# Own tiles, an early load and a new order around the rounding of the delta-rule outputs in a bidirectional hybrid block

## The chip, the cores and the metric

The kernel runs on one core of a Trainium2 chip. The metric is the device time of one execution in microseconds (us), given as the median of several runs. The engines are named as in the profile: PE is the matrix engine (TensorE), with PEld for its weight loads; DVE is VectorE, ACT is ScalarE, POOL is GpSimd, SP is SyncE. SP, ACT and POOL each have a queue in which they issue DMA transfers; in the profile, SPq and ACTq rows are such issues, while those of POOL stand under POOL. Every engine works through its own list of instructions in order. Where an instruction waits, everything behind it on that engine waits too.

## What is computed

The block takes 256 tokens of width 2048 (one sequence, one layer). It is an adaptive layer norm with a projection into two branches, a merge, an output projection and a gated feed-forward layer, all in float32. The part around the change, cut from the reference:

```python
mod = c_act @ ada_w + ada_b
shift_m, scale_m, gate_m, shift_f, scale_f, gate_f = jnp.split(mod[:, None, :], 6, axis=-1)
h = rms_norm(x, norm_mix_w) * (1 + scale_m) + shift_m
proj = h @ w_in
...
h_a = bidirectional(mlstm_chunkwise, (q_a, k_a, v_a), (log_i[0], log_f[0]), (log_i[1], log_f[1]))
h_a = rms_norm(h_a.transpose(0, 2, 1, 3), mlstm_norm_w.reshape(A_HEADS, A_DV)).reshape(bsz, t, A_V)
y_a = (jax.nn.sigmoid(a_o.astype(f32)) * h_a).astype(x.dtype) @ w_branch_a
...
o_b = bidirectional(gated_delta_chunkwise, (q_b, k_b, v_b), (beta[0], log_decay[0]), (beta[1], log_decay[1]))
o_b = rms_norm(o_b.transpose(0, 2, 1, 3), gdn_norm_w.reshape(B_HEADS, B_DV)).reshape(bsz, t, B_V)
y_b = (o_b * jax.nn.silu(b_z.astype(f32))).astype(x.dtype) @ w_branch_b

g_a, g_b = jnp.split(jax.nn.sigmoid(merge), N_BRANCH, axis=-1)
x = x + gate_m * ((g_a * y_a + g_b * y_b) @ w_out)
```

The mLSTM branch has 4 heads (keys of 256, values of 512), the gated delta rule 16 heads of 128.

## The kernel before

**Matmuls in two parts.** Every large weight is split into a rounded high part and a rest, `wh` and `wl`, and so is every activation (`hh` and `hl`, `obh` and `obl`, and so on). A product then takes three matmuls: high by high, low by high, high by low. ACT rounds (`wh`), DVE subtracts (`wl`). `tjob` (line 195) does this for weights with tokens as rows of the output: it loads 1 MB of weights per step `u` into one of three `raw` buffers by a DMA on SP, makes two halves of `wh` and `wl` of 128x1024 each (three buffers for each tag), and issues twelve matmuls per half (lines 230 to 232). Each call gives back control after each half, and so is a list of small pieces of work. `fjob` (line 169) does the same with tokens along the free axis.

**Filling.** The delta rule is a chain of small dependent steps. Its function `gdn_phase2` (line 745) handles a pair of heads and gives back control after each step; between the steps `fill` (line 265) and `stream` (line 883) issue pieces of the projections, so that PE has work. The adaLN products (`add`, line 118: one DVE instruction over 128x2048 for a block of `mod`) are dealt out in the same way.

**Planner and pins.** The instructions are traced in the order of the program. A scheduler then orders each engine's list by its own estimate of when an instruction's inputs are there and its buffers free, program order being the priority. So an instruction that stands later in the program may come earlier on its engine. `order(ins)` (line 72) pins one instruction behind the one traced before it on the same engine.

**Corrected outputs.** The last step of `gdn_phase2` transposes a pair's normalised outputs back (line 837), scales them into a tile `obt` of 128x256 (lines 840 and 841, ACT), and stores it to `ob_d` in DRAM by a DMA on ACT's queue (line 842). `obt` uses the tag "evf" of the pool `evp`, with two buffers; the evictions of the mLSTM's q and k (`keep_f`, line 355: `ev_a`, stored to `kq_d`) use the same two.

**mLSTM.** `mlstm(h)` (line 911) loads decays and q, k of a head (lines 915 and 917, POOL's queue), computes the scores and the decay matrix (lines 921 to 944; `psc` is the scores' product, line 930), then the denominators (line 958), and then the products by v for two blocks of 128 tokens (`ph`, line 974). For each token block and head there are three products, each of them two records in the trace; they go into two PSUM tiles of a tag `g` with four buffers. ACT scales the first (line 976), DVE adds the second (line 977), ACT squares and sums (line 978).

**The changeover.** After the last pair of the delta rule its pool `bk` is freed (line 1060). Pools of the next stage are opened in its place. Line 1116 loads the corrected outputs of groups 0 and 1, each 512 KB, by POOL's queue into two buffers `o4` of the pool `ml`. Then heads 0 and 1 of the mLSTM are driven on by `next(cores)`; `o_split` (line 1075) rounds a group's outputs into `obh` (ACT, 128x1024) and subtracts into `obl` (DVE), both pinned. The order by the program is: denominators; rounding of group 0, load of group 2, products by v of token block 0; rounding of group 1, load of group 3, products of token block 1; rounding of group 2. The branch projection `y_b` (line 1079) consumes group `g` in its weight step `u = g`. It begins with the load of a merge gate (`gtb`, 512 KB, line 1081, SP's queue, two buffers), which is read after its last matmul.

Of the kernel before, what the change touches and what calls it, by code (L numbers as in the profile page):

```python
# [9 lines left out]
F32 = mybir.dt.float32  # L10
F32R = mybir.dt.float32r
AF = mybir.ActivationFunctionType
ALU = mybir.AluOpType
PSUM = bass.MemoryType.PSUM

P = 128
T = 256
# [35 lines left out]
def hybrid_block(ctx: ExitStack, tc: tile.TileContext, xr, nfr, crow, pk_d, cst_d, ada2, ada4, win0, winb, wint, wba, wbb, wo, wgu, wd, out, dbg=None):  # L53
    nc = tc.nc
    V, S, G, PE = nc.vector, nc.scalar, nc.gpsimd, nc.tensor

    def pool(stack, name, bufs=1, **kw):
        return stack.enter_context(tc.tile_pool(name=name, bufs=bufs, **kw))
# [3 lines left out]
    rows_p = pool(ctx, "rows")  # L62
    acc_ps = pool(ctx, "acc_ps", 4, space=PSUM)
    g_ps = pool(ctx, "g_ps", 4, space=PSUM)
    sa, sx, sf = ExitStack(), ExitStack(), ExitStack()
    crp = pool(ctx, "crp")
    bigA = pool(sa, "bigA", 2, side="right")

# [3 lines left out]
    def order(ins, yes=True):  # L72

        return tc.keep_in_program_order(ins) if yes else ins

    def gps(name):
        return g_ps.tile([P, 512], F32, tag="g", name=name)
# [60 lines left out]
    def settle(keep=0, only=None):  # L138

        now = [f for f in behind if only is None or f.__name__ == only]  # L140
        for f in now[: len(now) - keep]:
            behind.remove(f)
            f()
# [143 lines left out]
    mb_d = [tc.dram_tile([P, 2, 512], F32, name=f"mb_d{g}") for g in range(4)]  # L287
    ob_d = [tc.dram_tile([4, P, T], F32, name=f"ob_d{g}") for g in range(4)]
# [6 lines left out]
    evp = pool(sa, "evp", side="right")  # L295
# [193 lines left out]
    with ExitStack() as s0:  # L489
        w0 = pool(s0, "w0")  # L490

        x = w0.tile([P, KB, T], F32, name="x")
        ss = w0.tile([P, 2], F32, name="ssx")
# [73 lines left out]
            fill(2 if i in (2, 3, 4, 6, 8, 9, 10) else 1)  # L567


    bk = pool(sx, "bk")  # L570
    own, nxt, half = cst[:, CS_OWN : CS_OWN + 4], cst[:, CS_NEXT : CS_NEXT + 4], cst[:, CS_HALF : CS_HALF + 2]
    even, odd = cst[:, CS_EVEN : CS_EVEN + 1], cst[:, CS_ODD : CS_ODD + 1]
# [172 lines left out]
    def gdn_phase2(g, p):  # L745
# [3 lines left out]
        hs = slice(2 * p, 2 * p + 2)  # L749
# [84 lines left out]
        for e, on in enumerate(ons):  # L834
            h, hl_ = 4 * g + 2 * p + e, 2 * p + e
            for t in range(2):
                PE.transpose(px[:, (2 * e + t) * P : (2 * e + t + 1) * P], on[:, t], ident)
        for e in range(2):
            h, hl_ = 4 * g + 2 * p + e, 2 * p + e
            obt = evp.tile([P, T], F32, tag="evf", bufs=2, name=f"obt{h}")  # L840
            S.activation(obt, px[:, e * T : (e + 1) * T], AF.Copy, scale=pk[:, PK_GNW + h : PK_GNW + h + 1])
            S.dma_start(ob_d[g][hl_], obt)
        yield
# [39 lines left out]
    def stream(h0):  # L883

        todo = []

        def piece():

            for q in list(todo):
                q[0] -= 1  # L890
                if not q[0]:
                    todo.remove(q)
                    next(heads1[q[1]])

        for h in range(h0, min(h0 + 2, NH_B)):
            for j in range(3):
                for _ in b_job(h, j):
                    piece()
                    yield True
            todo += [[2, h], [4, h]]  # L900
        while todo:
            fill(1)
            piece()
            yield True
        while True:
            fill(1)
            yield True

    mq, sq_ = {}, ExitStack()

    def mlstm(h):
        mp, load = mq["pool"], G
        bc = mp.tile([P, 2, T], F32, tag="bc", bufs=2, name=f"bc{h}")
# [45 lines left out]
        dn = ml.tile([P, 2, 2], F32, tag="dn", bufs=2, name=f"dn{h}")  # L959
# [4 lines left out]
        hs = ml.tile([P, 2, DV_A], F32, tag="hs", bufs=2, name=f"hs{h}")  # L964
        sq = ml.tile([P, DV_A], F32, tag="sqh", bufs=2, name=f"sqh{h}")
        ss = ml.tile([P, 2], F32, tag="ssh", bufs=2, name=f"ssh{h}")
        yield
        for t in range(2):
            pn = []
            for d in range(2):  # L970
                ph = gps(f"ph{h}_{t}_{d}")
                terms = src[d, t]
                for i, (w, s) in enumerate(terms):
                    PE.matmul(ph, w, vt[:, s], start=i == 0, stop=i == len(terms) - 1)
                pn.append(ph)
            S.activation(hs[:, t], pn[0], AF.Copy, scale=dn[:, t, 0:1])
            V.scalar_tensor_tensor(hs[:, t], pn[1], dn[:, t, 1:2], hs[:, t], ALU.mult, ALU.add)
            S.activation(sq, hs[:, t], AF.Square, accum_out=ss[:, t : t + 1])
            yield
        S.activation(ss, ss, AF.Sqrt, bias=epsc, scale=1.0 / DV_A)  # L980
        V.reciprocal(ss, ss)
# [3 lines left out]
        for e2 in range(2):  # L985
            px = gps(f"pxa{h}_{e2}")
            for e in range(2):
                f = 2 * e2 + e
# [33 lines left out]
    for g in range(4):  # L1022
        blocks = gdn_blocks(g)
        next(blocks)
        fill(7 if g else 8)
        next(blocks)
        fill(1)
        pairs = [gdn_phase2(g, p) for p in range(2)]
        if g == 3:
            settle()  # L1030
            sf.close()
            mq["pool"] = pool(sq_, "mq", side="right")
            first2 = [mlstm(h) for h in range(2)]
            for c in first2:
                next(c)
        every[0] = 1
        for p in range(2):
            pieces = stream(4 * g + 2 * p + 4)
            for n in range(1, 10):

                held[0] = n < 4
                if p == 0:
                    next(blocks, None)
                next(pairs[p], None)
                if g == 3 and n == (8, 4)[p]:
                    next(first2[p])
                for _ in range(last[n] if g == 3 else second[n] if p else after[n]):
                    next(pieces)
            for _ in pairs[p]:
                pass  # L1050

            if g < 3:
                while 4 * g + 2 * p + 5 not in heads:
                    next(pieces)
        if g < 3:
            fills.insert(0, z_job(g + 1))
            every[0] = owed[0] = 0
            invert(g + 1)
# [1 line left out]
    sx.close()  # L1060


    sc, sm_ = ExitStack(), ExitStack()
    pool(sc, "edgeC").tile([P, 56], F32, name="edgeC")
    bigC = pool(sc, "bigC", 2)
    gtp = pool(sc, "gtp")
    ml = pool(sm_, "ml")
    obh, obl = big(bigC, F32R, "obh"), big(bigC, F32R, "obl")

    def o_load(g):  # L1070
        o4 = ml.tile([P, 4, T], F32, tag="o4", bufs=2, name=f"o4_{g}")
        G.dma_start(o4, ob_d[g].rearrange("h p t -> p h t"))
        return o4

    def o_split(g, o4):
        order(S.activation(obh[:, 4 * g : 4 * g + 4], o4, AF.Copy))
# [1 line left out]

    def y_b(g):
        gt = gtp.tile([P, 2, 512], F32, tag="gt", bufs=2, name=f"gtb{g}")  # L1080
        nc.sync.dma_start(gt, mb_d[g])

        def done(ps):
            for t in range(2):
                V.tensor_tensor(mg[:, t, g * 512 : (g + 1) * 512], gt[:, t], ps[t], ALU.mult)
        return tjob(f"yb{g}", [wbb[g, u] for u in range(4)], obh, obl, done)

    def y_a(g):
# [24 lines left out]
        for g in range(4):  # L1113
            yield from y_b(g)

    o4s = [o_load(g) for g in range(2)]
    every[0] = owed[0] = 0
    held[0] = False
    cores = steps(*first2)
    fill(1)  # L1120
    next(cores)
    fill(2)
    for g in range(2):
        o_split(g, o4s[g])
        o4s.append(o_load(g + 2))
        next(cores)
    o_split(2, o4s[2])
    fill(1000)
    sq_.close()
# [259 lines left out]
    for j in range(FB // 4):  # L1389
# [4 lines left out]
        for e2 in range(2):  # L1394
            px = gps(f"pxf{j}_{e2}")
            for e in range(2):
                f = 2 * e2 + e
# [159 lines left out]
```

## Time and profile before

| | us |
|---|---|
| median of 3 runs | 1970.1 |
| lowest and highest | 1968.26, 1971.29 |
| the profiled execution's own time | 1969.12 |
| its span, first to last instruction | 1966.6 |
| PE busy in it | 1925.2 |
| mean granted clock of PE | 0.996 |

All times in the trace count from the span's start. A row of the timeline gives start, length, engine, line of the kernel, operation and tiles. Neighbouring instructions of one kind are merged (x12). Brackets at the end give the time for which the engine had been idle just before, and the instruction or transfer that released it. The projections and the delta rule fill the stretch to about 957 us, the changeover lies at 957 to 980, the branch projections, the merge and the feed-forward layer follow.

### The profile page before, as it was taken

The page shows a single profiled execution, that of the slowest core. Times are in us where ns is not written, and L with a number is a line of the kernel's source. Part 1 is how long each engine was busy: PE and PEld are TensorE (multiplying, and loading weights), DVE is VectorE, ACT ScalarE, POOL GpSimd, SP SyncE. Part 2 cuts the span into 40 slices and gives each one's busy share as a digit, 9 for nine tenths or more (in the row PEclk, how much of TensorE's full clock was granted, in tenths as well). Part 3 has the DMA queues.
Part 4 walks back from the last instruction along what each step waited for, and adds up shares of the span by engine and source line. Part 5 has one row for each costly group of instructions (what it writes and reads, how often), then busy time and mean ns, then how long its engine had stood idle before and what let it go on. Part 6 is the DMA issues. An engine that isn't in the chain of part 4 may idle for free. (4 is left out here: it accounts for less than half of the span.)

```text
span 1966.6 us, 27097 instructions
## 1 busy us (share of the span) xinstructions
PE 1925.2 (98%) x10418; PEld 1701.1 (86%) x10418; DVE 1406.0 (71%) x2067; ACT 1028.7 (52%) x1553; POOL 116.5 (6%) x211
## 2 busy tenths in 40 slices
PE   8999999999999999999999999999999999999998
PEld 6888889998999899888787888888888888888886
DVE  6779886887888799866577988765666665555554
ACT  3137656765776587564544444644444444444444
POOL 0001210111011101110100000200000000000000
PEclk9999999999999999999999999999999999999999
DMA  9986677667576766586686998566676665565554
GB/s 400 420 351 224 187 248 254 216 222 236 213 237 194 237 221 230 193 286 230 235 310 250 348 356 325 176 252 238 248 261 237 238 244 202 193 214 202 205 201 142
DMA packets 78962, 485.64 MB, mean 247 GB/s; under 512 B 10585, under 2 KB 15969, under 8 KB 24433
## 3 DMA queue, kind: packets, MB, share of 16 engines
q1 hardware_dynamic: 63216, 450.69, 63.0%
q0 software_dynamic: 8160, 17.88, 4.3%
q10 hardware_dynamic: 7458, 15.36, 2.1%
q8 instruction: 81, 1.33, 0.3%
q14 instruction: 47, 0.39, 0.1%
HBM read 467.07 MB, written 16.82 MB: 246 GB/s over the span
## 5 line engine op out<-in xcount | busy, mean ns | idle before, releaser
L211 DVE TENSOR_TENSOR wl_d<-raw_d,wh_d 128x1024 fp32r<-128x1024 f32 x88 | 107.6, 1224 | 105.9 <-ACT wh_d L209 105.9
L211 DVE TENSOR_TENSOR wl_up<-raw_up,wh_up 128x1024 fp32r<-128x1024 f32 x88 | 107.7, 1224 | 100.2 <-ACT wh_up L209 100.1
L211 DVE TENSOR_TENSOR wl_gt<-raw_gt,wh_gt 128x1024 fp32r<-128x1024 f32 x88 | 108.1, 1228 | 80.3 <-ACT wh_gt L209 80.3
L183 PE MATMUL acc_b<-hh,wh_b 128*128 128x256 f32 x576 | 161.8, 281 | 0.0
L209 ACT ACTIVATE wh_d<-raw_d 128x1024 fp32r<-128x1024 f32 x88 | 92.9, 1056 | 126.4 <-PE acc_d L231 117.6
L185 PE MATMUL acc_b<-hh,wl_b 128*128 128x256 f32 x576 | 158.7, 276 | 0.1
L184 PE MATMUL acc_b<-hl,wh_b 128*128 128x256 f32 x576 | 158.3, 275 | 0.0
L209 ACT ACTIVATE wh_gt<-raw_gt 128x1024 fp32r<-128x1024 f32 x88 | 92.9, 1055 | 118.6 <-PE acc_gt L231 71.1
L209 ACT ACTIVATE wh_up<-raw_up 128x1024 fp32r<-128x1024 f32 x88 | 92.7, 1055 | 108.1 <-PE acc_up L231 77.1
L123 DVE SCALAR_TENSOR_TENSOR ada<-ada,crow 128x2048 f32<-128x2048 f32 x64 | 146.1, 2283 | 0.0
L230 PE MATMUL acc_gt<-wh_gt,hfh 128*128 128x512 f32 x352 | 135.4, 385 | 0.6 <-ACT hfh L1344 0.6
L231 PE MATMUL acc_gt<-wh_gt,hfl 128*128 128x512 f32 x352 | 135.1, 384 | 0.0
L232 PE MATMUL acc_gt<-wl_gt,hfh 128*128 128x512 f32 x352 | 134.2, 381 | 0.0
L230 PE MATMUL acc_up<-wh_up,hfh 128*128 128x512 f32 x352 | 133.4, 379 | 0.0
L231 PE MATMUL acc_up<-wh_up,hfl 128*128 128x512 f32 x352 | 133.4, 379 | 0.0
L232 PE MATMUL acc_up<-wl_up,hfh 128*128 128x512 f32 x352 | 133.4, 379 | 0.0
L230 PE MATMUL acc_d<-wh_d,ffh 128*128 128x512 f32 x344 | 130.5, 379 | 0.0
L231 PE MATMUL acc_d<-wh_d,ffl 128*128 128x512 f32 x344 | 130.5, 379 | 0.0
L232 PE MATMUL acc_d<-wl_d,ffh 128*128 128x512 f32 x344 | 130.4, 379 | 0.0
L557 PE MATMUL first<-x,raw 128*128 128x256 f32 x512 | 114.5, 382 | 6.8 <-ACT x L551 6.3
L557 PEld LDWEIGHTS first<-x,raw 128*128 128x128 f32 x512 | 96.0, 190 | 25.3 <-ACT x L551 11.9
L184 PEld LDWEIGHTS acc_b<-hl,wh_b 128*128 128x128 f32 x576 | 110.6, 192 | 0.1
(383 smaller groups left out, 5257.5 us busy)
## 6 DMA issues: line engine op xcount, KB each, us to landing
ada<-ada SPq DMA_DIRECT2D x64, 1024.0 KB, 6.1
raw_gt<-wgu SPq DMA_DIRECT2D x44, 1024.0 KB, 4.9
raw_up<-wgu SPq DMA_DIRECT2D x44, 1024.0 KB, 4.9
raw_d<-wd SPq DMA_DIRECT2D x44, 1024.0 KB, 4.8
raw_b<-winb SPq DMA_DIRECT2D x36, 1024.0 KB, 5.6
ra<-ada SPq DMA_DIRECT2D x32, 1025.0 KB, 15.7
raw<-win SPq DMA_DIRECT2D x16, 1024.0 KB, 14.6
raw_z<-wint SPq DMA_DIRECT2D x16, 1024.0 KB, 4.9
```

The lines of the kernel that those rows point to most:

```text
L123: order(V.scalar_tensor_tensor(raw, raw, 1.0, row_c[:, :D], ALU.mult, ALU.mult, accum_out=mod[:, c : c + 1]))
L183: PE.matmul(o, wh[:, k], woven(hh[:, kk]), start=kk == 0, stop=False)
L184: PE.matmul(o, wh[:, k], woven(hl[:, kk]), start=False, stop=False)
L185: PE.matmul(o, wl[:, k], woven(hh[:, kk]), start=False, stop=kk == KB - 1)
L209: order(S.activation(wh, raws[u][:, k0 : k0 + 2], AF.Copy), early)
L211: order(V.tensor_tensor(wl, raws[u][:, k0 : k0 + 2], wh.bitcast(F32), ALU.subtract), early)
L230: order(PE.matmul(ps[t], xh[:, kk, c], woven(wh[:, k]), start=kk == 0, stop=False), early and steps > 1)
L231: PE.matmul(ps[t], xl[:, kk, c], woven(wh[:, k]), start=False, stop=False)
L232: PE.matmul(ps[t], xh[:, kk, c], woven(wl[:, k]), start=False, stop=kk == last)
L557: PE.matmul(first[o], raw[:, o], x[:, b], start=b == 0 and o % 2 == 0, stop=b == KB - 1 and o % 2 == 1)
```

## The change

Four things are different. Corrected outputs get a pool of their own, `obp`, with two buffers; it is opened before the delta rule's pool and lives on below it. The load of group 0's corrected outputs moves into `mlstm`'s first pool, with one buffer, behind the first loads of heads 0 and 1; only groups 1, 2 and 3 use the two buffers in `ml`. The scaling, adding and squaring of heads 0 and 1 is pinned, and the products of token block 0 stand ahead of the rounding of group 0, those of block 1 ahead of the rounding of group 1. The load of a merge gate moves from the front of `y_b` behind its third half of matmuls, and is pinned there on SP's queue.

```diff
+    obp = pool(sc, "obp")
     bk = pool(sx, "bk")
...
-            obt = evp.tile([P, T], F32, tag="evf", bufs=2, name=f"obt{h}")
+            obt = obp.tile([P, T], F32, tag="obt", bufs=2, name=f"obt{h}")
...
+    def o_load(g, home):
+        o4 = home.tile([P, 4, T], F32, tag="o4", bufs=2 if g else 1, name=f"o4_{g}")
+        G.dma_start(o4, ob_d[g].rearrange("h p t -> p h t"))
+        return o4
...
-            S.activation(hs[:, t], pn[0], AF.Copy, scale=dn[:, t, 0:1])
-            V.scalar_tensor_tensor(hs[:, t], pn[1], dn[:, t, 1:2], hs[:, t], ALU.mult, ALU.add)
-            S.activation(sq, hs[:, t], AF.Square, accum_out=ss[:, t : t + 1])
+            order(S.activation(hs[:, t], pn[0], AF.Copy, scale=dn[:, t, 0:1]), h < 2)
+            order(V.scalar_tensor_tensor(hs[:, t], pn[1], dn[:, t, 1:2], hs[:, t], ALU.mult, ALU.add), h < 2)
+            order(S.activation(sq, hs[:, t], AF.Square, accum_out=ss[:, t : t + 1]), h < 2)
...
             for c in first2:
                 next(c)
+            o4s = [o_load(0, mq["pool"])]
...
     def y_b(g):
         gt = gtp.tile([P, 2, 512], F32, tag="gt", bufs=2, name=f"gtb{g}")
-        nc.sync.dma_start(gt, mb_d[g])
...
+        for n, x in enumerate(by(g, done)):
+            if n == 2:
+                order(nc.sync.dma_start(gt, mb_d[g]))
+            yield x
+
+    def by(g, done):
         return tjob(f"yb{g}", [wbb[g, u] for u in range(4)], obh, obl, done)
...
-    o4s = [o_load(g) for g in range(2)]
+    o4s.append(o_load(1, ml))
...
     fill(1)
     next(cores)
     fill(2)
+    next(cores)
     for g in range(2):
         o_split(g, o4s[g])
-        o4s.append(o_load(g + 2))
-        next(cores)
+        o4s.append(o_load(g + 2, ml))
+        if not g:
+            next(cores)
     o_split(2, o4s[2])
     fill(1000)
```

More of the change, by code (lines that the diff above doesn't have):

```diff
@@ L64, in hybrid_block @@
     g_ps = pool(ctx, "g_ps", 4, space=PSUM)
-    sa, sx, sf = ExitStack(), ExitStack(), ExitStack()
+    sa, sc, sx, sf = ExitStack(), ExitStack(), ExitStack(), ExitStack()
     crp = pool(ctx, "crp")
@@ L1060, in hybrid_block @@
     sx.close()
-    sc, sm_ = ExitStack(), ExitStack()
+    sm_ = ExitStack()
     pool(sc, "edgeC").tile([P, 56], F32, name="edgeC")
@@ L1068, in hybrid_block @@
     obh, obl = big(bigC, F32R, "obh"), big(bigC, F32R, "obl")
[L1070 to L1073, printed above, removed]
     def o_split(g, o4):
```

## Prediction

> **What bounds the kernel now.** I read the page first, then who TensorE waited for, then the two places where it waited longest, in order of time.
>
> ```profile
> span 1966.6 us, 27097 instructions
> PE 1925.2 (98%) x10418; PEld 1701.1 (86%) x10418; DVE 1406.0 (71%) x2067; ACT 1028.7 (52%) x1553; POOL 116.5 (6%) x211
> ```
>
> ```profile
> PE ph L974 <- ACT hs L976: 3.9, 1, 3.9
> PE p L791 <- DVE pt L780: 3.9, 2, 2.5
> ```
>
> TensorE is busy for 98% of the span, so a change pays only where it idles (1966.6 - 1925.2 = 41 us) or runs slowly. In its list of waits (sum, times, longest), the two longest single ones that other engines cause are these: 3.9 us ahead of the mLSTM products by v, and 2.5 us ahead of a step of the delta rule's inversion (lines 780 and 791). The change touches what lies behind both.
>
> **Place one, the rounding of corrected outputs** (timeline: start, length, engine, line, in brackets the idle time and its releaser):
>
> ```profile
> 956.59 0.80 SPq L1081 DMA_DIRECT2D gtb<-mb_d  x2
> 957.05 1.51 POOL L1072 DMA_DIRECT2D o<-ob_d  x2 [58.69 <-ACT ev_ma L351]
> 958.95 5.40 PE L974 MATMUL ph<-vt,mdec 128*128 128x512 f32 x12
> 966.60 1.06 ACT L1076 ACTIVATE obh<-o 128x1024 fp32r<-128x1024 f32 x1 [7.30 <-DMA o<-ob_d]
> 967.57 0.67 ACT L976 ACTIVATE hs<-ph,dn 128x512 f32<-128x512 f32 x1
> 967.69 1.22 DVE L1077 TENSOR_TENSOR obl<-o,obh 128x1024 fp32r<-128x1024 f32 x1 [7.92 <-ACT obh L1076]
> 968.29 7.02 PE L974 MATMUL ph<-vt,mdec 128*128 128x512 f32 x12 [3.94 <-ACT hs L976]
> 968.84 0.74 DVE L977 SCALAR_TENSOR_TENSOR hs<-ph,dn,hs 128x512 f32<-128x512 f32 x1
> 969.65 0.62 ACT L978 ACTIVATE sqh<-hs 128x512 f32<-128x512 f32 x1
> 970.17 0.20 ACT L978 ACTIVATION_READ_ACCUMULATOR sqh<-hs 128x1 f32 x1
> 974.75 0.78 PE L230 MATMUL acc_yb<-wh_yb,obh 128*128 128x512 f32 x1
> 975.36 0.38 PE L231 MATMUL acc_yb<-wh_yb,obl 128*128 128x512 f32 x1
> 975.58 0.38 PE L232 MATMUL acc_yb<-wl_yb,obh 128*128 128x512 f32 x1
> ```
>
> The loads of group 0 and 1 start only at 957.05, when memory of the delta rule comes free. ACT's queue has the rounding of group 0 (966.60) ahead of the first scaled product (967.57), so ACT sits 7.30 us on a transfer while the product it could take has been ready since about 960. The first twelve product records fill all four PSUM buffers of their tag; the next twelve need one back, and TensorE stops for 3.94.
>
> **Place two, the coupled small buffers:**
>
> ```profile
> 903.78 0.36 ACT L358 ACTIVATE ev_a<-acc_a 128x256 f32<-128x256 f32 x1
> 908.79 0.47 ACT L841 ACTIVATE obt<-px,pk 128x256 f32<-128x256 f32 x1 [1.88 <-DMA kq_d<-ev_a]
> 908.80 0.82 ACTq L842 DMA_DIRECT2D ob_d<-obt  x2
> 914.52 0.38 ACT L358 ACTIVATE ev_a<-acc_a 128x256 f32<-128x256 f32 x1 [3.72 <-DMA ob_d<-obt]
> 916.24 1.10 ACT L787 ACTIVATE UL<-p 32x128 f32<-32x128 f32 x4
> 916.27 1.10 PE L779 MATMUL p<-X,cc 128*128 128x64 f32 x8 [0.44 <-ACT X L773]
> 917.37 1.06 ACT L178 ACTIVATE wh_a<-raw_a 128x1024 fp32r<-128x1024 f32 x1
> 918.46 1.23 DVE L180 TENSOR_TENSOR wl_a<-raw_a,wh_a 128x1024 fp32r<-128x1024 f32 x1 [6.40 <-ACT wh_a L178]
> 919.61 2.29 DVE L123 SCALAR_TENSOR_TENSOR ada<-ada,crow 128x2048 f32<-128x2048 f32 x1
> 921.82 0.68 DVE L780 TENSOR_TENSOR pt<-p,cst 128x512 f32<-128x512 f32 x1
> 922.56 1.10 PE L791 MATMUL p<-X,pt 128*128 128x64 f32 x8 [2.45 <-DVE pt L780]
> 923.50 3.46 PE L930 MATMUL psc<-mkq 128*128 128x256 f32 x8
> 926.40 0.77 PE L183 MATMUL acc_a<-hh,wh_a 128*128 128x256 f32 x1
> ```
>
> Corrected outputs (obt) and evictions (ev_a) share the two "evf" buffers. An obt waits 1.88 for the store of an eviction, so both obt stores leave late (908.80), and the next eviction waits 3.72 for one of them. From 914.52 on ACT works without a break, so all behind it is late by about that: the rounding at 917.37, DVE's subtraction at 918.46, the adaLN product of 2.29 that is queued next, and only then pt, whose input TensorE had delivered by 917.4. TensorE stands still from 920.11 to 922.56.
>
> Both stops are followed by a low granted clock. In the table by stretches stand the length and the busy time of PE, its weight loads, DVE, ACT and POOL; the last three numbers are granted clock, DMA share and GB/s. The two rows under them are an undisturbed run of psc:
>
> ```profile
> 920.00:923.00 3.00, 0.55 (x5) 0.45 (x5) 3.00 (x4) 1.06 (x1) 0.00 (x0) 1.00 0.78 217
> 923.00:927.00 4.00, 4.00 (x16) 3.32 (x16) 3.94 (x7) 0.38 (x1) 0.00 (x0) 0.60 1.01 411
> 968.00:972.00 4.00, 3.71 (x5) 1.70 (x6) 3.37 (x4) 2.96 (x7) 0.76 (x1) 0.57 0.92 303
> 895.64 1.89 PE L930 MATMUL psc<-mkq 128*128 128x256 f32 x8
> 897.18 0.46 PE L183 MATMUL acc_a<-hh,wh_a 128*128 128x256 f32 x1
> ```
>
> **The change, part by part.** Own obt tiles (line 840). No instruction comes or goes; 1.88 and 3.72 of ACT's waits lose their cause. The eviction then needs only the buffer of an earlier eviction, and follows the rounding before it at about 910.8, 3.7 earlier. In the same order, UL ends near 913.6, the rounding runs to 914.7, DVE's subtraction to 915.9, the adaLN product to 918.2, pt to 918.9. TensorE, without its 0.44 at 916.27, reaches L791 at 920.11 - 0.44 = 919.67, so 0.75 is left and the stop goes. Gain: 0.44 + 2.45, and the slow stretch: the eight psc records take 926.40 - 923.50 = 2.90 instead of 897.18 - 895.64 = 1.54, that is 1.36, and some 0.27 in the next two. Together **4.5**. The ends: 0 if pt stays late for another reason, 4.5 if it is in time. I take 4.5, since each link of the chain has its row.
>
> The Trainium skill, "TensorE: Matmul & The Clock Gate", section "What's actually happening", has the clock fall after a free-running idle window of about 3.4 us. Here a stop of 2.45 was followed by 0.60. By the rule this stop would have cost only itself and the sum would be 1.6 smaller; the row decides.
>
> Early load of group 0 and products ahead of the rounding. The first rounding no longer waits for a transfer; the products' chain is pinned ahead of it on ACT and DVE (lines 976 to 978, heads 0 and 1). How long one record of ph takes (shortest, median, longest, in ns):
>
> ```profile
> L974 PE MATMUL ph<-vt,mdec x48: 592/592/1222, 958.9 to 1052.7; 128*128 128x512 f32 x48
> ```
>
> The records are (5.40 - 0.59) / 11 = 0.44 apart, so twelve take 5.25. Undisturbed, the second twelve start at 958.95 + 5.25 = 964.2 instead of 968.29, a gain of 4.1. They take 5.25 instead of 974.75 - 968.29 = 6.46, 1.2 more. The first product of the branch projection takes 0.2 instead of 0.61, at most 0.4. Together **5.7**.
>
> What takes the place of that wait. Behind the pinned chain on ACT stand the rounding, weight roundings and a square root with its table. I lay the chain out on the old clock: head 0's second product is there at 961.6; DVE 0.74, square and its read 0.8: 963.2; head 1's scaling, ready second product (964.4), DVE, square: 965.9; obh of group 0 to 967.0, obl to 968.2. TensorE ends the products at 969.45, so group 0 is in time by 1.2. The second token block goes the same way: 967.7, DVE 968.9 behind obl, square 969.8, head 1 970.5, 971.2, 972.0, then obh of group 1 to 973.1 and obl to 974.3. TensorE has consumed group 0 (24 records, 0.215 apart) at 969.65 + 5.16 = 974.8. The margin is 0.5, and ACT has other work for these gaps:
>
> ```profile
> 975.80 1.28 ACT L980 ACT_TABLE_LOAD   x1
> 977.10 0.29 ACT L980 ACTIVATE ssh<-ssh,epsc 128x2 f32<-128x2 f32 x1
> ```
>
> The root and its table aren't pinned and can come as soon as head 0's squares are done: 1.28 + 0.29 - 0.5 = 1.1 of new wait; with one weight rounding too, 1.06 more, and then 1.6 of slow clock as at place two: 3.7. The ends are 0 and 3.7; I take **1.2**, near the row of one table load.
>
> The Trainium skill, "ScalarE: Activation LUTs", section "What ACT_TABLE_LOAD costs", adds a drain of about 1.4 us to each load of 1.28, which would speak against this order: the new wait would be 2.6. No such gap stands between 975.80 and 977.10; the row decides.
>
> Loads that move. Group 0's load is issued by POOL at about 854 instead of 957:
>
> ```profile
> 853.93 0.54 POOL L938 DMA_DIRECT2D vt<-v_d  x1
> 840.00:880.00 40.00, 39.59 (x200) 34.68 (x199) 25.57 (x33) 24.81 (x41) 8.44 (x15) 1.00 0.86 302
> ```
>
> Only vt stands behind it, used first at 958.95: nothing. Its 512 KB are 1.7 us of transfer at 302 GB/s in a stretch where TensorE idles 0.41; three weight buffers hide it, otherwise it costs up to 1.7. The loads for group 2 find a free buffer, so they leave at about 958 instead of 969. The merge-gate loads (gtb) are pinned behind their projection's second weight load on SP's queue. From there five steps of 12 records (5 x 2.6 = 13 us) remain until they are read, against at most 9.5 for a landing (957.05 to 966.60, group 0's in a crowded stretch), and weight loads queued behind one wait only 0.4 for its issue (0.80 for two): nothing. If late, they'd hold DVE, not TensorE, which has two more accumulators.
>
> **Sum.** The profiled execution takes 1969.12, 2.5 beyond its span. 1969.1 - 4.5 - 5.7 + 1.2 = 1960.1. The median of the three runs, 1970.1, lies 1.0 above; I forecast **1960**.
>
> **Rivals.** *B, only place one gains.* The new allocation lets pt stay behind the adaLN product and the subtraction (both 918.46 to 921.8), say since weight roundings fill ACT's 3.7. For it: DVE was busy 3.00 of 3 from 920 on. Against it: DVE idled 6.40 just before. 1969.1 - 5.7 + 1.2 = 1964.6.
>
> *C, ACT is the new bound of place one.* The wait for obl of group 1 reaches its full 3.7: 1969.1 - 10.2 + 3.7 = 1962.6. For it: ACT was busy 2.96 of 4 there already. Against it: it gets the gaps of 959 to 966, where it idled 7.30, for the same work.
>
> *D, slower.* The eight pairs' obt no longer hold ACT back, so the planner deals all engines' order anew from the first pair on; where DVE gets an adaLN product (2.29) ahead of a pair's pt, TensorE stops as at 922.56, each time 4.5. It decides from three of the eight pairs: 1960.1 + 13.5 = 1973.6. For it: the list has two such waits at L791 now. Against it: only one reached 2.45, and that one needed ACT's 3.72 ahead of it.
>
> **How the numbers follow.** The forecast gets 0.58, B 0.14, C 0.11, D 0.09; 0.08 remains for one pair of D's kind on top of B, 1964.6 + 4.5 = 1969, no change. What can be told from no change here is 0.2%, 4 us. Faster are the first three, 0.83, less a little for their upper ends: 0.82; same 0.09; slower 0.09. The forecast's own range is 1958.9 (no new wait) to 1962.6. The range of 8 in 10 goes down to 1957 for the short waits of ACT for evf elsewhere, and up to 1967.5, beyond B with the early load's 1.7.
>
> **What would show it.** The 3.72 before ev_a and the 2.45 before L791 are gone; psc takes 1.5 again; ACT scales ph about 960, ahead of obh; the second ph records follow without a gap, in 5.3; the branch projection starts near 965 (974.75 less 9 to 10). A wait of TensorE for obl before group 1 measures the new term. Wrong would be: pt still behind an adaLN product with TensorE waiting (B), this wait over 2 us (C), or new stops before L766 and L791 in earlier pairs (D).

## The result, and the profile after

| | before | after |
|---|---|---|
| median of 9 runs (us) | 1969.96 | 1960.51 |
| lowest and highest | 1964.15, 1974.65 | 1957.58, 1962.88 |
| ratio of after to before, 95% interval | | 0.9952 (0.9940 to 0.9964) |
| the profiled execution's own time | 1969.12 | 1962.84 |
| its span | 1966.6 | 1961.0 |
| mean granted clock in it | 0.996 | 0.994 |

The changed kernel is faster by 0.48%, 9.5 us in the medians. The profiled execution of it is the second slowest of its nine, 2.3 above their median, so the two profiles differ by less, 5.6 us of span. What this execution lost by a low clock is shown at the end of this section. First come the head of the page and TensorE's list of waits (sum, times, longest) of the changed kernel:

```profile
span 1961.0 us, 27095 instructions
PE 1926.3 (98%) x10418; PEld 1703.2 (87%) x10418; DVE 1405.7 (72%) x2067; ACT 1028.7 (52%) x1553; POOL 116.9 (6%) x211
```

```profile
PE first L557 <- ACT x L551: 7.5, 15, 2.4
...
PE p L767 <- DVE pt L759: 1.2, 1, 1.2
```

Both waits that the prediction started from, 3.9 ahead of the products by v and 2.5 ahead of a step of the inversion, are gone from the list, and none has come for corrected outputs. What is left of the list stands far from the two places; the 1.2 at line 767 is at 378 us. The other wait at line 791 in the old list, 1.5 at 753 us, is gone too, but it isn't a gain of the own buffers: with the buffers shared again (e1, below) it is 0.24. All lines of the changed file are some higher: 792 is the old 791, 937 the old 930, 965 the old 958, 981 the old 974, 983 to 985 the old 976 to 978, 987 the old 980, 1079 and 1080 the old 1076 and 1077; 914 is the load that was in line 1072.

**Place two.** The timeline of the changed kernel (start, length, engine, line, tiles; in brackets idle time and releaser):

```profile
913.20 0.37 ACT L358 ACTIVATE ev_a<-acc_a 128x256 f32<-128x256 f32 x1
914.91 1.11 ACT L788 ACTIVATE UL<-p 32x128 f32<-32x128 f32 x4
916.04 1.06 ACT L178 ACTIVATE wh_a<-raw_a 128x1024 fp32r<-128x1024 f32 x1
917.13 1.23 DVE L180 TENSOR_TENSOR wl_a<-raw_a,wh_a 128x1024 fp32r<-128x1024 f32 x1 [2.54 <-ACT wh_a L178]
918.27 2.28 DVE L123 SCALAR_TENSOR_TENSOR ada<-ada,crow 128x2048 f32<-128x2048 f32 x1
920.48 0.69 DVE L781 TENSOR_TENSOR pt<-p,cst 128x512 f32<-128x512 f32 x1
921.98 1.00 PE L792 MATMUL p<-X,pt 128*128 128x64 f32 x8
922.82 1.95 PE L937 MATMUL psc<-mkq 128*128 128x256 f32 x8
924.41 0.46 PE L183 MATMUL acc_a<-hh,wh_a 128*128 128x256 f32 x1
```

The eviction of 913.20 has no bracket: its wait is gone. The order behind it is the old one, UL, rounding, subtraction, adaLN product, pt, only earlier: pt ends at 920.48 + 0.69 = 921.17 and TensorE comes for it at 921.98. There is no stop, and the eight psc records take 924.41 - 922.82 = 1.59 instead of 2.90.

How much that is worth is read from the same instruction in both traces, ahead of the place and behind it. Ahead of it, first the kernel before, then the changed one:

```profile
858.30 0.48 PE L232 MATMUL acc_mb<-wl_mb,hh 128*128 128x512 f32 x1 [0.41 <-DVE wl_mb L211]
```

```profile
861.03 0.48 PE L232 MATMUL acc_mb<-wl_mb,hh 128*128 128x512 f32 x1 [0.78 <-DVE wl_mb L211]
```

**Place one**, the timeline of the changed kernel:

```profile
805.56 0.78 POOL L914 DMA_DIRECT2D o<-ob_d  x1 [0.20 <-issue]
956.59 10.55 PE L981 MATMUL ph<-vt,mdec 128*128 128x512 f32 x24
957.73 0.69 ACT L983 ACTIVATE hs<-ph,dn 128x512 f32<-128x512 f32 x1 [0.79 <-PE ph L981]
963.50 1.04 ACT L1079 ACTIVATE obh<-o 128x1024 fp32r<-128x1024 f32 x1
966.57 0.78 PE L230 MATMUL acc_yb<-wh_yb,obh 128*128 128x512 f32 x1
967.19 0.38 PE L231 MATMUL acc_yb<-wh_yb,obl 128*128 128x512 f32 x1
967.80 1.28 ACT L987 ACT_TABLE_LOAD   x1
967.82 0.75 DVE L984 SCALAR_TENSOR_TENSOR hs<-ph,dn,hs 128x512 f32<-128x512 f32 x1 [1.36 <-ACT hs L983]
969.30 0.61 ACT L985 ACTIVATE sqh<-hs 128x512 f32<-128x512 f32 x1
969.91 1.99 ACT L1079 ACTIVATE obh<-o 128x1024 fp32r<-128x1024 f32 x2
970.99 2.36 DVE L1080 TENSOR_TENSOR obl<-o,obh 128x1024 fp32r<-128x1024 f32 x2
972.37 0.38 PE L231 MATMUL acc_yb<-wh_yb,obl 128*128 128x512 f32 x1
```

The 24 records of ph are one unbroken row of the timeline now, where there were two of twelve with 3.94 between. ACT scales the first product at 957.73, and the rounding of group 0 (963.50) stands in the middle of the chain. The load of group 0 was issued at 805.56 and had 150 us to land.

So, by the same instructions in both traces: at 858 the changed kernel is 2.7 late; at the first ph it is at 956.59 against 958.95, 2.36 early. Place two gave 2.73 + 2.36 = **5.1**. At the first product of the branch projection it is at 966.57 against 974.75, 8.18 early. Place one gave 8.18 - 2.36 = **5.8**. Together 10.9.

**What the profiled execution lost.** Two stretches of the changed kernel (length; busy time of PE, weight loads, DVE, ACT, POOL; clock, DMA share, GB/s), then what stands right ahead of each in the timeline; then, of the kernel before, the first stretch and what stands ahead of it:

```profile
380.00:384.00 4.00, 4.00 (x20) 4.00 (x20) 3.73 (x7) 2.23 (x8) 1.60 (x4) 0.50 0.66 195
1020.00:1024.00 4.00, 4.00 (x13) 3.20 (x12) 1.04 (x2) 0.97 (x1) 0.00 (x0) 0.57 0.94 389
```

```profile
378.37 1.46 PE L767 MATMUL p<-R,pt 128*128 128x32 f32 x7 [1.17 <-DVE pt L759]
1016.55 2.73 PE L965 MATMUL pden<-ones,mdec 128*128 128x1 f32 x24
```

```profile
380.00:384.00 4.00, 4.00 (x38) 4.00 (x38) 3.84 (x7) 2.95 (x10) 1.70 (x4) 1.00 0.65 199
```

```profile
378.49 1.08 PE L766 MATMUL p<-R,pt 128*128 128x32 f32 x8 [1.17 <-DVE pt L758]
```

Both kernels stop for the same 1.17 at 378. Before, the clock stays at 1.00 behind it; after, it is granted at 0.50, and 20 records get through where 38 did. The four microseconds ahead of this window have 0.83 and the four behind it 0.81, so the low clock costs 4 x (0.17 + 0.50 + 0.19) = 3.4, more than the whole 2.7 that the changed kernel is late at 858. At 1020 the clock is 0.57 for four microseconds though TensorE waited for nothing: 4 x (1 - 0.57) = 1.7 lost. What stands ahead of it is 2.73 us of single-column products, the mLSTM's denominators. With these two, the 10.9 come down to 10.9 - 3.4 - 1.7 = 5.8, against 5.6 between the spans. (A third difference is at 1245.6 to 1252.5, behind stops of 1.5 and 1.0 that both kernels have: the clock is 0.51 there for 6.9 us, where it is low for 3.4 in the kernel before. It costs at most 1.7, and something of that size elsewhere must make up for it; what, remains open.) All these losses are behind the change's two places or far ahead of them; the experiments show whether they belong to the change.

### The profile page after: what moved, and what is told of

Its sections match the earlier page's. It is cut to its first block, busy times and chain, and to the rows that moved or that the text cites. A ratio compares the mean times of both kernels' runs of the same rounds, so it can differ in the third digit from the quotient of the medians.

```text
span 1961.0 us, 27095 instructions
## 1 busy us (share of the span) xinstructions
PE 1926.3 (98%) x10418; PEld 1703.2 (87%) x10418; DVE 1405.7 (72%) x2067; ACT 1028.7 (52%) x1553; POOL 116.9 (6%) x211
## 4 chain that ended last, share of the span: by engine, by line
PE 83%; DVE 7%; DMA 6%; ACT 2%; issue 2%; POOL 0%; SPq 0%; ACTq 0%; DVEq 0%; POOLq 0%
PE acc_gt L230 4%; PE acc_gt L231 4%; PE acc_gt L232 4%; PE acc_up L232 4%; PE acc_up L231 4%; PE acc_up L230 4%; PE acc_d L232 4%; PE acc_d L231 4%; PE acc_d L230 4%; DMA ra<-ada 3%; PE acc_b L183 3%; PE acc_b L185 3%; PE acc_b L184 3%; PE acc_o L232 3%; PE acc_o L230 3%; PE acc_o L231 2%
## 5 line engine op out<-in xcount | busy, mean ns | idle before, releaser
L183 PEld LDWEIGHTS acc_b<-hh,wh_b 128*128 128x128 f32 x576 | 111.9, 194 | 0.1
```

What stands on the lines that cost most here:

```text
L183: PE.matmul(o, wh[:, k], woven(hh[:, kk]), start=kk == 0, stop=False)
```

## The experiments

The theory that was tested is the prediction's: two stops, each with a cause of its own in ACT's order, and no more. The rivals were, in turn, that a part of the edit does nothing (the early load, the new order or the gate loads), that place two's gain has another cause, and that the low clock at 1020 is a price of the change. "Ratio" is to the kernel before on the same chip.

| run | median (us) | lowest, highest | ratio, 95% interval |
|---|---|---|---|
| e1, changed, obt shared again | 1962.80 | 1959.35, 1964.06 | 0.9960 (0.9945 to 0.9975) |
| e2, before, with own obt only | 1966.81 | 1962.99, 1969.06 | 0.9984 (0.9974 to 0.9994) |
| e3, changed, late load | 1961.71 | 1959.71, 1963.95 | 0.9958 (0.9943 to 0.9972) |
| e4, changed, old order | 1962.00 | 1959.98, 1964.52 | 0.9959 (0.9945 to 0.9974) |
| e5, changed, gate loads first | 1960.25 | 1957.38, 1962.25 | 0.9946 (0.9933 to 0.9959) |
| e6, e1 with an adaLN product held | 1958.79 | 1955.89, 1962.76 | 0.9940 (0.9926 to 0.9954) |
| e7, changed, denominators twice | 1970.23 | 1966.50, 1974.88 | 0.9999 (0.9989 to 1.0009) |
| e8, changed, second denominators apart | 1957.49 | 1956.25, 1959.91 | 0.9934 (0.9921 to 0.9946) |
| e9, changed, both denominators apart | 1960.78 | 1958.12, 1962.04 | 0.9952 (0.9940 to 0.9965) |
| e10, changed, late load and old order | 1963.63 | 1961.45, 1964.51 | 0.9969 (0.9956 to 0.9982) |
| e11, the changed kernel again | 1958.50 | 1955.86, 1961.71 | 0.9944 (0.9931 to 0.9957) |

Runs e1 to e4 shared one chip, e5 to e8 a second, e9 to e11 a third; the kernel before took 1970.62, 1970.00 and 1969.31 on them. One kernel's executions scatter over 4 to 8 us, so a median tells some 2 us at best, and the place itself is read in the trace.

**Shared obt (e1).** The changed kernel, with the corrected outputs back in the evictions' buffers:

```diff
-    obp = pool(sc, "obp")
...
-            obt = obp.tile([P, T], F32, tag="obt", bufs=2, name=f"obt{h}")
+            obt = evp.tile([P, T], F32, tag="evf", bufs=2, name=f"obt{h}")
```

> The changed kernel, but corrected outputs share the two buffers of the mLSTM evictions again. My theory: two stops with separate causes, so the gain of place two alone is lost. TensorE waits some 2.5 us for pt at the step of line 792 again, with a slow clock behind it; place one stays mended (the 24 ph records in one run of 10.5 us). Time 1960.5 + 4.5 = 1965, span some 4.5 to 5 above the changed kernel's. Rival (the new order around the changeover moves the whole plan, and the buffers have nothing to do with it): time stays at 1960.5 and no wait at line 792.

The timeline of e1:

```profile
912.30 0.39 ACT L358 ACTIVATE ev_a<-acc_a 128x256 f32<-128x256 f32 x1 [3.50 <-DMA ob_d<-obt]
920.34 1.24 PE L791 MATMUL p<-X,pt 128*128 128x64 f32 x8 [2.45 <-DVE pt L780]
921.37 3.54 PE L936 MATMUL psc<-mkq 128*128 128x256 f32 x8
```

The whole chain is back: the eviction waits 3.50 for an obt store, TensorE stops for 2.45, and psc runs at the low clock. In the median this is only 2.3 above the changed kernel's 1960.5, and their intervals overlap, so the median confirms the mechanism and not the size of 4.5. The trace does better: at the product that stood at 861.03 in the changed kernel e1 is at 856.36, 4.67 early, and it starts the denominators at 954.13 against 953.99, 0.14 late. In between it lost 4.8.

**Own obt alone (e2).** The opposite: the kernel before, with nothing but the new pool and the two lines above reversed.

> The kernel before, with nothing but own buffers for corrected outputs. My theory: place two is mended, place one is not. ACT's 3.7 us before ev_a and TensorE's 2.45 before L792 are gone, the 3.9 us ahead of the second ph records stay. Time 1970 - 4.5 = 1965.5. Rival (an earlier place two only runs into a longer wait at the changeover, which loads nothing earlier): the wait ahead of ph grows and the time stays within 2 us of before, 1968 to 1970.

The timeline of e2:

```profile
919.87 1.00 PE L792 MATMUL p<-X,pt 128*128 128x64 f32 x8
962.33 1.06 ACT L1077 ACTIVATE obh<-o 128x1024 fp32r<-128x1024 f32 x1 [7.24 <-DMA o<-ob_d]
964.02 7.11 PE L975 MATMUL ph<-vt,mdec 128*128 128x512 f32 x12 [2.47 <-ACT hs L977]
```

Place two is mended and place one is not. It gains 3.8 (1970.62 - 1966.81), near the 4.5. By the same instructions in the traces it is 0.61 late at 858 (858.91 against 858.30) and 4.47 early at the denominators (951.88 against 956.35), a gain of 5.1. The stop at place one is only 2.47 in this execution, since the first twelve products had run at a low clock and taken 6.81 instead of 5.40.

**The adaLN product (e6).** Of place two's chain one link was left to be tried: does ACT's late rounding make TensorE stop by itself, or only with the adaLN product queued between it and pt? e6 is e1 with that product held back for two more steps of the last pair:

```diff
-                held[0] = n < 4
+                held[0] = n < (6 if g == 3 and p else 4)
```

> The kernel of the first experiment (shared buffers, the rest changed) in which adaLN products are held back for two more steps of the last pair. My theory: ACT still waits 3.5 us for the store of an obt, but the stop of TensorE needs the adaLN product of 2.29 us between the subtraction and pt as well; without it pt is ready at about 918, and the wait of 2.45 at line 791 shrinks to 0.3 or goes: 1960.5 to 1961.5, so 1 to 2 us below the first experiment's 1962.8. Rival (ACT's delay alone makes the stop): the wait stays above 1.5 us and the time at 1962.8.

The timeline of e6:

```profile
914.43 0.39 ACT L358 ACTIVATE ev_a<-acc_a 128x256 f32<-128x256 f32 x1 [3.60 <-DMA ob_d<-obt]
919.52 0.68 DVE L780 TENSOR_TENSOR pt<-p,cst 128x512 f32<-128x512 f32 x1
920.26 1.10 PE L791 MATMUL p<-X,pt 128*128 128x64 f32 x8 [0.24 <-DVE pt L780]
```

ACT waits as long as before, 3.60, but pt now stands directly behind the subtraction, and 0.24 of TensorE's 2.45 remains. The stop needed both: a store that holds ACT, and 2.29 of a product without haste on DVE. With the buffers shared, this other repair is as fast as the change (1958.79).

**Late load (e3), old order (e4), neither (e10).** The change mends place one in two ways at once. e3 takes back the early load (three buffers in `ml`, group 0 loaded there), e4 the order and its pins, e10 both:

```diff
-        o4 = home.tile([P, 4, T], F32, tag="o4", bufs=2 if g else 1, name=f"o4_{g}")
+        o4 = home.tile([P, 4, T], F32, tag="o4", bufs=3, name=f"o4_{g}")
...
-            o4s = [o_load(0, mq["pool"])]
...
-    o4s.append(o_load(1, ml))
+    o4s = [o_load(g, ml) for g in range(2)]
```

```diff
     fill(2)
-    next(cores)
     for g in range(2):
         o_split(g, o4s[g])
         o4s.append(o_load(g + 2, ml))
-        if not g:
-            next(cores)
+        next(cores)
```

(and in `mlstm` the three `h < 2` of the pins become `False`).

> The changed kernel, but group 0's load leaves at the changeover again (three buffers there, so that the later loads are not delayed). The order of products and rounding stays new. My theory: the products no longer stop, but group 0's rounding now meets its transfer (issued near 954.7, 9.5 us as before: 964.3, then 1.0 and 1.2 us for obh and obl: 966.6), so TensorE, ready at 966.6, waits 0 to 2 us: time 1960.5 to 1963. Rival (the early load is what pays, the order is nothing): the stop of 4 us with its slow clock is back, 1966.

> The changed kernel, but with the old order at the changeover: rounding of group 0 ahead of the products of token block 0, rounding of group 1 ahead of those of block 1, nothing of the products' chain pinned. Group 0 is still loaded early. My theory: the early load alone takes the 7.3 us wait out of ACT's queue, so the first products are scaled at once and TensorE doesn't stop; group 1's transfer may hold ACT up behind the first block's scaling, where nothing of the first blocks depends on it: 1960.5, at most 1962. Rival (the order is what pays): ACT stands at a rounding ahead of the scalings, TensorE stops 2 us or more ahead of ph, 1963 to 1966.

> The changed kernel with both repairs of place one undone: group 0 loaded at the changeover (three buffers) and rounding ahead of the products, nothing pinned. Each undone alone cost at most 1.5 us. Theory (either one suffices): with neither, ACT's 7 us wait for group 0's transfer is back ahead of the first scaling and TensorE stops 2.5 to 4 us ahead of the second ph records: 1960.5 + 4 to 5.7, so 1964.5 to 1966. Rival (place one gained through something else, such as the gates' loads that stay moved): no such stop, 1961 to 1962.

The timelines of e3, of e4 and of e10:

```profile
951.71 1.52 POOL L914 DMA_DIRECT2D o<-ob_d  x2 [53.59 <-ACT ev_ma L351]
953.60 12.24 PE L981 MATMUL ph<-vt,mdec 128*128 128x512 f32 x24
962.20 1.04 ACT L1078 ACTIVATE obh<-o 128x1024 fp32r<-128x1024 f32 x1
```

```profile
954.59 10.55 PE L981 MATMUL ph<-vt,mdec 128*128 128x512 f32 x24
955.15 1.06 ACT L1079 ACTIVATE obh<-o 128x1024 fp32r<-128x1024 f32 x1 [0.21 <-ACT dn L967]
```

```profile
961.17 1.06 ACT L1078 ACTIVATE obh<-o 128x1024 fp32r<-128x1024 f32 x1 [6.27 <-DMA o<-ob_d]
962.86 7.11 PE L981 MATMUL ph<-vt,mdec 128*128 128x512 f32 x12 [2.91 <-ACT hs L983]
```

With the new order alone (e3) the load is issued at 951.71 and the rounding, at its place behind the first products, finds the data there. With the early load alone (e4) the rounding stands ahead of everything at 955.15 and has its data, so it costs ACT only its 1.06. In both, ph is one unbroken row. In e3 this row is 12.24 long and not 10.55, since the clock was low in it (0.51 from 954.2 to 957.7), and that gave the load 1.7 us more. Without it the rounding would have come at 962.2 - 1.7 = 960.5. A transfer of 8.5 us, as e10 had it (952.66 to 961.17), lands at 960.2, one of 9.5, as before, at 961.2; even then obl would be done at 961.2 + 1.0 + 1.2 = 963.4, ahead of the product that reads it (965.90 - 1.7 = 964.2). That is an estimate; no run shows e3's place one at full clock. With neither (e10) ACT waits 6.27 and TensorE stops for 2.91. So **either repair removes the stop by itself**, and the second adds nothing that these runs can tell: e3 and e4 lie 1.2 and 1.5 above the changed kernel's 1960.5, within its scatter. On one chip, e10 is 5.1 above the changed kernel (1963.63 against 1958.50, with intervals that just touch): that is place one's size by medians. In e10's trace it takes 969.41 - 954.55 = 14.9 from the first ph to the first product of the branch projection, against 10.0 in the changed kernel, so 4.9.

**Gate loads (e5).** The changed kernel, with the load of a merge gate at the front of `y_b` again:

```diff
-        for n, x in enumerate(by(g, done)):
-            if n == 2:
-                order(nc.sync.dma_start(gt, mb_d[g]))
-            yield x
+        nc.sync.dma_start(gt, mb_d[g])
+        yield from by(g, done)
```

> The changed kernel, but the merge gates' loads stand at the front of their projections again and are not pinned. My theory: this move was worth nothing, since the loads are read 13 us after their new place and no engine waited for them: 1960.5 to 1961.5, no wait of TensorE between 945 and 1000 us. Rival (a second 512 KB load at the changeover delays group 1's transfer, behind which ACT holds the rounding of group 1): TensorE waits 1 to 3 us for obl in the first branch projection, 1962 to 1964.

It took 1960.25 against 1960.51, and TensorE waited for nothing between 945 and 1000, as in the changed kernel. The move is worth nothing that these runs can tell.

**The low clock behind the denominators (e7, e8, e9).** One theory: a row of 24 single-column products looks to the clock like idleness, and behind it the clock falls by chance, whatever the change did. The rival: 1020 is a consequence of the change's new order. e7 issues the denominators twice (the second results are not read); e8 issues those of heads 2 and 3 apart, with a half of the branch projection between; e9 does this for heads 0 and 1 as well.

```diff
-        for (d, t), terms in src.items():
-            for i, (w, s) in enumerate(terms):
-                PE.matmul(pd_[:, 2 * t + d : 2 * t + d + 1], w, ones1, start=i == 0, stop=i == len(terms) - 1)
+        for again in (0, 4):
+            for (d, t), terms in src.items():
+                c = again + 2 * t + d
+                for i, (w, s) in enumerate(terms):
+                    PE.matmul(pd_[:, c : c + 1], w, ones1, start=i == 0, stop=i == len(terms) - 1)
```

```diff
-    drive(steps(mlstm(2), mlstm(3)), 3)
+    two = [mlstm(h) for h in (2, 3)]
+    for _ in range(2):
+        for c in two:
+            next(c)
+        fill(3)
+    next(two[0])
+    fill(1)
+    next(two[1])
+    fill(2)
+    drive(steps(*two), 3)
```

(e8 has, beside this, the two `next` of heads 0 and 1 written out with a `fill(1)` behind each; in its trace their denominators are still one row. In e9 the first product by v of head 0 stands between them.)

> The changed kernel with the single-column products of the denominators issued twice (the second results are not read): 24 more records of 0.11 us per pair of heads, 2.6 us, for two pairs 5.2 us. Theory: the matrix engine's clock control takes these products, 2.7 us in a row, for near idleness, and falls by chance (in four of six profiles so far it was low behind the second of the two places, in two behind the first, without any wait of TensorE); at 5.4 us in a row it falls every time. The profile shows clock below 0.9 behind both places, each costing some 1.7 us: 1960.5 + 5.2 + 2 x 1.7 less the 1.7 that it costs on average now, 1967.5. Rival (the low clock has nothing to do with these products): 1965.7, and at most one place with a low clock.

> The changed kernel, but the denominators of heads 2 and 3 are issued apart, with a half of projection matmuls (2.6 us) between the two runs of 1.4 us; those of heads 0 and 1 stay one run of 2.7. Theory of the clock control: no low clock at 1015 to 1030 us any more, 1.7 us times its share of executions (two of three): 1959.4. At the first place, nothing changes. Rival: the low clock there comes as often as before, 1960.5.

> As the kernel with the denominators of heads 2 and 3 apart, and now those of heads 0 and 1 too: head 0's products by v of the first token block stand between them. No run of single-column products is longer than 1.4 us. Theory of the clock control: no low clock at 948 to 964 us either, where four of nine profiles of kernels with 24 records in a row had one of 1.7 us; all executions at a mean clock of 0.996 or more, 1957 us; the products by v take 10.5 us plus 2.7 for the denominators between them, without a wait. Rival (the first place's low clock has another cause, such as the turn of the stage): it comes in about half of the executions as before, 1957.5 to 1958.

Stretches of e7, and the timeline of its denominators with the first products behind them; then the denominators of heads 2 and 3 in e8 and the stretches behind:

```profile
956.00:964.00 8.00, 8.00 (x18) 4.22 (x19) 1.97 (x6) 2.54 (x6) 0.00 (x0) 0.63 0.99 388
1020.00:1028.00 8.00, 8.00 (x49) 7.64 (x50) 3.17 (x9) 0.89 (x3) 0.00 (x0) 0.71 0.48 168
```

```profile
950.92 6.45 PE L967 MATMUL pden<-ones,mdec 128*128 128x1 f32 x48
957.24 12.86 PE L983 MATMUL ph<-vt,mdec 128*128 128x512 f32 x24
1019.50 6.73 PE L967 MATMUL pden<-ones,mdec 128*128 128x1 f32 x48
```

```profile
1012.57 1.40 PE L965 MATMUL pden<-ones,mdec 128*128 128x1 f32 x12
1016.50 1.40 PE L965 MATMUL pden<-ones,mdec 128*128 128x1 f32 x12
```

```profile
1016.00:1020.00 4.00, 4.00 (x27) 3.65 (x26) 1.55 (x4) 1.23 (x2) 0.00 (x0) 1.00 0.87 344
1020.00:1024.00 4.00, 4.00 (x18) 3.15 (x17) 1.23 (x1) 2.01 (x2) 0.00 (x0) 1.00 0.50 164
```

With 48 in a row the clock is low behind both places, with no wait of TensorE at either. The kernel takes 9.7 more than the changed one, more than either theory had given it. The rows say where: the denominators are (6.45 - 2.73) + (6.73 - 2.73) = 7.7 longer and the first products by v 12.86 - 10.55 = 2.3, so the clock is low within the long rows too and not only behind them. With twelve and twelve (e8) it stays at 1.00. e9 had no low clock at either place, but new waits of 0.38 and 0.65 for weights at 982 and 984, and is not faster than the changed kernel beside it. e8 has the best median of all, but against the changed kernel its interval overlaps (0.9921 to 0.9946 beside 0.9931 to 0.9957 for e11): a gain is possible and not shown.

**The changed kernel again (e11).**

> The changed kernel itself, beside the other two on the same chip, so that they can be compared with it and not only with the kernel before: 1960.5 within 1.5 us; mean clock between 0.993 and 0.997 from one execution to the next, the longer times at the lower clock.

The stretch with the end of the same denominators (the last starts at 1014.5) and what is behind them, in e11:

```profile
1012.00:1020.00 8.00, 8.00 (x50) 7.36 (x49) 4.79 (x10) 2.60 (x5) 0.00 (x0) 1.00 0.79 296
```

This execution of the very same kernel has no low clock at 378 or at 1020 (1.00 from 372 to 386 and from 1010 to 1030); its span is 1954.0 against 1961.0 and it took 1955.86. The losses of the profiled execution differ from one execution to the next and are not a price of the change.

Over the profiles of before, after and e1 to e11, the clock fell behind a row of 24 denominators in 10 of 21 places: in 4 of 11 at the first place (e2, e3, e5, e6) and in 6 of 10 at the second (after, e1, e3, e4, e5, e6). The kernel before has the same rows of 24 and the clock did not fall behind either of them in its one profile. Behind a row of twelve it fell in none of 6, behind 48 in both.

The clock records of these traces also show what separates the 10 from the 11. Every spell of low clock ahead of the last matmuls lasts 3.41 us or twice that, at 0.50, and within one execution all of them begin at multiples of 3.413 us from each other, to 0.02 us: in the changed kernel at 378.68, 1020.38 and 1245.66, which are 188 and 66 steps apart. So each execution has a grid of steps, which lies differently against the program each time. At the 10 places where the clock fell, one step held 2.21 us or more of the row (up to all 2.74); at the 11 others no step held more than 2.03. Rows of twelve put at most 1.40 into a step, rows of 48 fill one. So what looks like chance goes with where the row lies on the grid; by an estimate from these numbers (a limit of 2.1) that hits a row of 2.73 in (2.73 - 2.1) + (3.41 - 2.1) = 1.9 of 3.41 positions, a little over half.

## Why the prediction was right

The forecast was 1960, the median is 1960.5; its mechanism, two stops that both go, is what the traces show. That the number came within 0.5 is in part luck, as the terms show:

- **Place two, 4.5: measured 5.1 in the trace**, 4.8 and 5.1 in those of e1 and e2, 3.8 by e2's medians. Two links of the chain were tried: shared buffers bring the stop back (e1), own ones alone remove it (e2), and the adaLN product is a necessary link (e6). The laid-out chain had pt ready 0.75 ahead of TensorE; it was 921.98 - 921.17 = 0.8. In the trace the low clock behind the stop went with it, which is 1.3 of the gain in psc alone (2.90 to 1.59), as the prediction had it from the row.
- **Place one, 5.7: measured 5.8 in the trace**, 4.9 in e10's, 5.1 by e10 against e11 in medians. Two of its small parts were off and cancel. The products by v take 966.57 - 956.59 = 10.0, 0.5 less than laid out; the first branch product still takes 967.19 - 966.57 = 0.62, so the 0.4 counted there did not come.
- **That early load and new order belong together** was taken without being tested: the prediction costs them in one term. They are two repairs of one stop, and either suffices (e3, e4). A sum with a term for each would have counted one gain twice.
- **The new wait, 1.2: measured 0.** This is the one term that was mis-sized. The table load came where the prediction put it, in the chain ahead of the rounding of group 1 (967.80). But for its first 0.77 ACT would have stood idle anyway: the square behind it needs DVE's addition, which ends at 967.82 + 0.75 = 968.57. The prediction added the whole 1.28 + 0.29 to the chain. obl of group 1 ended at about 970.99 + 2.36/2 = 972.2, and the product that reads it started at 972.37. The margin was 0.2, not the -1.1 laid out. The root moved that square from 968.57 to 969.30, so it cost 0.7 of its 1.57; the other 0.4 of the difference is that the chain without the root was laid out too long (a margin of 0.5 against 0.2 + 0.73 = 0.9). What is left is so small that what comes behind it on ACT still matters.
- **Gate loads, 0: right** (e5). **The early load's transfer, 0: right**; TensorE waits 1.05 and 0.78 for weights between 805 and 862, and 1.03 and 0.78 in e3, which has no such load there. It was issued at 805.56, 48 us earlier than the 854 laid out: on POOL's list it stands ahead of the loads of heads 0 and 1, which it follows in the program.
- **Rivals.** B (pt stays behind the adaLN product, TensorE waiting): the order stayed, the wait did not. C (ACT the new bound): no wait for obl. D (new stops in earlier pairs): none; the 1.17 at line 767 is in both traces. The second of two waits at line 791 that D cited is no gain of the buffers (0.24 in e1).
- **What the sum owes to luck.** With the measured gains and no new wait the sum is 1969.1 - 5.1 - 5.8 = 1958.2, or 1959.1 from the median of before, 1969.96. The measured median is 1.4 to 2.3 above that, so the 1.2 of a wait that did not come covered part of it. The profiled execution's 1962.8 and e11's 1955.9 show how far low-clock spells move one execution; that they also make up the 1.4 in the median is not shown.

## What to carry to other kernels

When an engine that works in order waits on a transfer, look at what is queued behind it, not at the transfer: here a store held an eviction on ACT, that held a rounding, that a subtraction and an unhurried product on DVE, and only then came the tile that TensorE needed. Here each of two stops went by either of two cuts (own buffers or the product held back; the early load or the new order), so an edit that makes both cuts gains once; try each alone before keeping both. Compare the same instruction ahead of the place and behind it in two traces, since the whole span also carries low-clock spells that cost 1.7 or 3.4 us each and fall elsewhere in the next execution.

## What the hardware showed that was not expected

TensorE's clock falls without any stop of TensorE. Behind 24 single-column products in a row (2.7 us, all of it counted as busy) it was low in 10 of 21 places, behind 48 (6.5 us) in both, behind twelve (1.4 us) in none of six. What told these places apart was how much of the row lay in one step of a 3.41 us grid that lies differently in each execution: 2.21 us or more at all 10, 2.03 or less at the other 11. A spell is one or two steps at half the clock and costs 1.7 or 3.4. The stop of 1.17 at 378 was followed by one in 7 of the 13 profiles. This is probably much of why one kernel's executions scatter: the nine of the changed kernel range from a mean clock of 0.997 and 1957.58 us to 0.993 and 1962.88 us.

The Trainium skill, "TensorE: Matmul & The Clock Gate", section "What's actually happening", has the clock set by how busy the array was in free-running windows of about 3.4 us, and the low state come after an idle window. The traces agree with free-running windows: their grid has steps of 3.41 us and lies differently in each execution. Two things here don't follow from an idle window of that length: episodes behind rows and stops shorter than it, and that a row which the profile counts as busy acts as idleness, 2.2 us of it in a window being enough. The runs do not show how the chip weighs such narrow products; that they count for little is an inference from e7, e8 and the grid.
